# First stage's attention of a two-block model on one core: heads in three steps, and the out projection accumulated per pair of heads

## The chip, the core and the metric

The kernel runs on one core of a Trainium2 chip. The metric is the device time of one execution in microseconds (us), as the median of several runs. TensorE (PE) multiplies matrices into PSUM (eight banks of 128 x 512 fp32 each), ScalarE (ACT) and VectorE (DVE) work on elements, GpSimd (POOL) helps, and SyncE (SP) issues most loads from memory.

## The reference

256 tokens of width 1024 pass a first block of two layers (latent attention "mla", then gated linear attention "gla", each followed by a PEER layer with 16384 experts) and a second block with two kinds of windowed attention and a feed-forward layer. The change is in the first layer's attention:

```
def mla_mixer(x, positions, w_down, g_q_lat, w_uq, g_kv_lat, w_ukv, g_qn, g_kn, w_o):
    down = x @ w_down
    c_q, c_kv = rms_norm(...), rms_norm(...)          # 384 and 256 wide
    q = (c_q @ w_uq).reshape(B, S, 16, 96)
    kv = (c_kv @ w_ukv).reshape(B, S, 16, 64 + 64)
    k = concatenate([kv[..., :64], broadcast(k_rope)], axis=-1)
    v = kv[..., 64:]
    q, k = rms_norm and rope of both
    o = causal_attention(q, k, v)                      # 16 heads, 256 queries, blocks of 128
    return o.reshape(B, S, 16 * 64) @ w_o
h = h + mix;  h = h + peer_ffn(rms_norm(h, ...), ...)
```

## The kernel before

Activations lie transposed, features on partitions and 256 tokens along the free axis; h is 8 rows of 128 features. Most products are made in three passes of fp32r: each operand is split into a high and a low part (`split`: ACT writes hi as a copy, DVE writes lo as the rest), and hi x hi, hi x lo and lo x hi are added in PSUM (`mm3`, lines 109 to 111). A weight block of 512 KB is loaded by SP into a tile raw and split (`wblock`); raw, hi and lo have three buffers each (pool strm, line 32). PSUM is two pools of four banks: tag mm (`c.psum()`) and tag acc (`c.psum_a()`, `c.pa`).

The instructions of an engine don't run in the order of the code: at compile time a planner with a model of the times orders them, earlier code first among those that it holds ready, and hands out free buffers as it goes. `behind` and `c.after` add orders by hand.

`mla` projects down, then K (line 791 makes k_), then Q, whose last products are followed by V's projection (24 passes of 512 columns). k_ is scaled per head by a pass (L880) and a DVE multiplication (L882). Then, per head h: four PE instructions make the scores S (L945 adds the mask in bf16, L947 multiplies in fp32, which the trace shows as two records each), DVE takes two maxima (L953), ACT two exponentials (L959), DVE the reciprocal and the scaling (L961, L964), PE three transposes (L967), ACT copies them to PT (L969), and PE multiplies by V (L971 and L973), with 64 columns of V as weights, into the half of a bank of tag acc that belongs to the head. Per pair of heads m, `split` makes row m of ohi and olo. After all heads, `out_proj` goes over the 8 rows of h: 8 x 3 passes of 256 columns each, then DVE adds to h (L680). Two of the eight blocks of w_o have buffers of their own (woh, wol).

Then the PEER layer begins (`peer_body`): `gain_split` (L136 on ACT, L137 on DVE) makes hi and lo of each row of h, and `proj_first` projects them with the first two blocks of wq at once:

```
    w01 = [c.wblock(wq[h], 1024, 5 + h) for h in range(2)]     # 545; its split stands behind row 5 (6) of gain_split
    c.gain_split(g, ghi, glo)
    p01 = [c.psum_a() for _ in range(2)]
    c.proj_first([p[:, :T] for p in p01], w01, (ghi, glo))
```

The class Accumulate stands in the kernel before too, where the last stage (ffn) alone uses it; its four banks are those of tag acc. `add` makes the 24 passes of one block (lines 234 to 236), but holds the last two blocks (LAST = 2) for `finish`:

```
        c.order = [0, 2, 4, 6, 1, 3, 5, 7]                     # 248
        for i, m in enumerate(c.order):
            for t in self.held:
                self.mm(m, *t)
            a = nc.vector.tensor_tensor(c.h[:, m], c.h[:, m], self.acc[m // 2][:, m % 2], op=OP.add)
            if i >= 2 and out is None:
                c.after[c.order[i - 2]] = [a.ins]
```

Of the kernel before, what the change touches and what calls it, by code (L numbers as in the profile page):

```python
# [5 lines left out]
F32 = mybir.dt.float32  # L6
# [707 lines left out]
def mla(c, v, a):  # L714

    nc, tc = c.nc, c.tc
    with tc.tile_pool(name="mla", bufs=1, reuse_waits="tile") as P:
# [168 lines left out]
        for j, jj in enumerate((4, 0, 1, 5, 2, 3)):  # L886
            w = c.wblock(a["w_uq"][jj], 768)
            for e in range(2):
# [25 lines left out]
                c.tick()  # L914

        V = P.tile([128, 2, 1024], F32, name="V", tag="gsq")
        ws = [c.wblock(a["w_ukv_v"][k], 1024) for k in range(2)]
        for b in range(2):
            for hf in range(2):
                p = c.psum()  # L920
                for k in range(2):
                    t = slice(b * 128, (b + 1) * 128)
                    s = slice(hf * 512, (hf + 1) * 512)
                    c.mm3(p, (lhi[:, 3 + k, t], llo[:, 3 + k, t]), (ws[k][0][:, s], ws[k][1][:, s]), k == 0, k == 1)
                nc.scalar.activation(V[:, b, hf * 512:(hf + 1) * 512], p, AF.Copy, scale=skv[:, b:b + 1])
                c.tick()
        c.tick(9)
        rqh = c.rstd(P, pss[:, :32].rearrange("p (b h) -> p b h", b=2), 96, "rqh", s=sq_, extra=96.0 ** -0.5)

        done = []  # L930
        c.table(AF.Exp, [c.last_sqrt])

        ohi, olo = (P.tile([128, 8, T], F32R, name=n) for n in ("ohi", "olo"))
        for m in range(8):
            po = c.pa.tile([128, 512], F32, name="acc", tag="acc")
            for e in range(2):
                h = 2 * m + e
                r = slice(e * 64, (e + 1) * 64)
                rq = slice(0, 128 if e else 96)
                S = c.psum()  # L940
                for qb in range(2):
                    tq = slice(qb * 128, (qb + 1) * 128)
                    n = 128 * (qb + 1)
                    o = S[:, qb * 128:qb * 128 + n]
                    nc.tensor.matmul(S[:, 256 * qb:256 * qb + 128], identb, cmask, start=True, stop=False,  # L945
                                     skip_group_check=True)
                    nc.tensor.matmul(o, q[rq, h, tq], k_[rq, h, :n], start=False, stop=True, skip_group_check=True)  # L947
                st = P.tile([128, 6], F32, name="st", bufs=6)
                Pm = P.tile([128, 384], F32, name="Pm", bufs=4)
                for qb in range(2):  # L950
                    n = 128 * (qb + 1)
                    sl = slice(qb * 128, qb * 128 + n)
                    nc.vector.tensor_reduce(st[:, qb:qb + 1], S[:, sl], axis=AX.X, op=OP.max)  # L953
                for qb in range(2):
                    n = 128 * (qb + 1)
                    sl = slice(qb * 128, qb * 128 + n)
                    nc.vector.scalar_tensor_tensor(st[:, 2 + qb:3 + qb], st[:, qb:qb + 1], -1.0, rqh[:, qb, h:h + 1],
                                                   op0=OP.mult, op1=OP.mult)
                    nc.scalar.activation(Pm[:, sl], S[:, sl], AF.Exp, bias=st[:, 2 + qb:3 + qb],  # L959
                                         scale=rqh[:, qb, h:h + 1], accum_out=st[:, 4 + qb:5 + qb])  # L960
                nc.vector.reciprocal(st[:, 4:6], st[:, 4:6])  # L961
                for qb in range(2):
                    sl = slice(qb * 128, qb * 256 + 128)
                    nc.vector.tensor_scalar(Pm[:, sl], Pm[:, sl], st[:, 4 + qb:5 + qb], None, op0=OP.mult)  # L964
# [634 lines left out]
```

## Time and profile before

| | |
|---|---|
| time before, median of 3 runs (lowest, highest) | 2219.31 us (2217.12, 2219.76) |
| the profiled execution, whole | 2215.98 us |
| its span, first to last instruction | 2214.2 us |
| instructions in it | 41185 |
| the attention with the out projection, on PE | about 64 to 129 us of the span |

A profile is one execution, recorded by the hardware. Times in rows are counted from the start of its span. PEld is TensorE's loading of weights, which overlaps its multiplications. The end of a matmul in a row is modelled, so that rows of PE overlap; the starts tell how fast it goes.

### The profile page before, as it was taken

The numbers are of one execution on the slowest core, as the hardware profiler recorded it, in microseconds if no ns is written. First come the engines' busy times: TensorE is split into PE (matmuls) and PEld (weight loads), VectorE is DVE, ScalarE is ACT, GpSimd is POOL, SyncE is SP. The second block draws the span as 40 slices with busy tenths as digits, with TensorE's granted clock in tenths as the row PEclk, the third lists the DMA queues.
The fourth block names the chain that finished last, engine by engine and source line by source line (L and its number), as shares of the span: only waits on it lengthen the run. The fifth ranks groups of instructions, "written<-read, shape, count | busy, mean of one in ns | idle before, by whom it ended". The sixth has DMA issues, their size and how long they took to land.

```text
span 2214.2 us, 41185 instructions
## 1 busy us (share of the span) xinstructions
PE 2188.5 (99%) x15545; PEld 2005.4 (91%) x15545; DVE 1654.6 (75%) x4268; ACT 1174.5 (53%) x1984; POOL 173.5 (8%) x243
## 2 busy tenths in 40 slices
PE   8999999999999999999999999999999999999999
PEld 7799999999888888889999999988888888779999
DVE  7779997888555777667999788865577767657665
ACT  7764554555554555566455455555445456445443
POOL 4100000111000111000000011100011132000000
PEclk9999999999999999999999999999999999999999
DMA  4254555555655777445455555565567766305554
GB/s 163 67 191 163 192 190 191 200 196 201 228 193 197 235 242 239 152 142 173 166 188 191 191 196 199 198 232 192 197 226 242 244 181 211 113 33 187 187 185 153
DMA packets 116168, 413.22 MB, mean 187 GB/s; under 512 B 14256, under 2 KB 16120, under 8 KB 115456
## 3 DMA queue, kind: packets, MB, share of 16 engines
q1 hardware_dynamic: 102960, 370.46, 48.9%
q0 software_dynamic: 12176, 39.43, 5.6%
q8 instruction: 122, 2.00, 0.4%
q10 hardware_dynamic: 832, 0.70, 0.1%
q14 instruction: 78, 0.64, 0.1%
HBM read 390.06 MB, written 19.94 MB: 185 GB/s over the span
## 4 chain that ended last, share of the span: by engine, by line
PE 93%; DMA 3%; ACT 2%; DVE 1%; issue 1%; ACTq 0%; SPq 0%; DVEq 0%
PE mm L109 16%; PE mm L111 16%; PE mm L110 16%; PE acc L274 10%; PE acc L272 10%; PE acc L273 10%; PE acc L480 1%; PE acc L481 1%; PE acc L109 1%; PE acc L110 1%; PE acc L111 1%; PE acc L235 1%; PE acc L236 1%; PE acc L234 1%; DMA raw<-in_w_qk 1%; PE mm L1351 1%
## 5 line engine op out<-in xcount | busy, mean ns | idle before, releaser
L94 ACT ACTIVATE hi<-raw 128x1024 fp32r<-128x1024 f32 (+1 forms) x687 | 725.8, 1057 | 850.8 <-PE mm L110 303.2
L95 DVE TENSOR_TENSOR lo<-raw,hi 128x1024 fp32r<-128x1024 f32 (+1 forms) x687 | 839.4, 1222 | 352.3 <-ACT hi L94 349.8
L110 PE MATMUL mm<-x,hi 128*128 128x256 f32 x2856 | 798.8, 280 | 3.1 <-DVE x L137 3.1
L109 PE MATMUL mm<-x,hi 128*128 128x256 f32 x2792 | 790.1, 284 | 7.8 <-ACT x L136 6.5
L111 PE MATMUL mm<-x,lo 128*128 128x256 f32 x2792 | 779.9, 280 | 0.0
L110 PEld LDWEIGHTS mm<-x,hi 128*128 128x128 f32 x2856 | 536.9, 188 | 3.9 <-DVE x L137 3.4
L109 PEld LDWEIGHTS mm<-x,hi 128*128 128x128 f32 x2792 | 524.4, 188 | 11.4 <-ACT x L136 6.5
L111 PEld LDWEIGHTS mm<-x,lo 128*128 128x128 f32 x2792 | 524.8, 188 | 0.0
L274 PE MATMUL acc<-hi,ws 128*128 128x512 f32 x992 | 385.9, 389 | 0.0
L273 PE MATMUL acc<-lo,ws 128*128 128x512 f32 x992 | 385.9, 389 | 0.0
L272 PE MATMUL acc<-hi,ws 128*128 128x512 f32 x992 | 266.1, 389 | 0.0
L274 PEld LDWEIGHTS acc<-hi,ws 128*128 128x128 f32 x992 | 186.2, 188 | 38.7
L272 PEld LDWEIGHTS acc<-hi,ws 128*128 128x128 f32 x992 | 186.2, 188 | 38.5
L273 PEld LDWEIGHTS acc<-lo,ws 128*128 128x128 f32 x992 | 186.2, 188 | 38.6
L441 DVE SCALAR_TENSOR_TENSOR Gs<-iota,Gs 128x17 f32<-128x17 f32 (+1 forms) x480 | 96.4, 255 | 0.9
L484 DVE SCALAR_TENSOR_TENSOR Hs<-acc,Hs 128x256 f32<-128x256 f32 x128 | 53.9, 421 | 54.3 <-PE acc L481 54.3
L519 POOL DMA_DIRECT2D ht<-spill x64 | 46.4, 725 | 600.1 <-DVE wm L521 568.0
L500 POOL DMA_DIRECT2D spill<-ht x64 | 46.6, 728 | 496.4 <-ACT ht L499 496.4
L480 PE MATMUL acc<-oh 128*128 128x128 f16 x512 | 67.7, 220 | 0.0
L485 ACT ACTIVATE Gs<-acc 128x192 f32<-128x192 f32 x128 | 41.9, 327 | 47.3 <-DVE Hs L484 47.3
L481 PE MATMUL acc<-oh 128*128 128x128 f16 x512 | 66.1, 218 | 0.0
L95 DVE TENSOR_TENSOR ws<-Hs,ws 128x256 fp32r<-128x256 f32 x128 | 52.8, 418 | 1.0 <-ACT ws L94 1.0
(450 smaller groups left out, 2867.5 us busy)
## 6 DMA issues: line engine op xcount, KB each, us to landing
raw<-in_u SPq DMA_DIRECT2D x256, 512.0 KB, 3.5
raw<-in_v SPq DMA_DIRECT2D x256, 512.0 KB, 4.3
spill<-ht POOLq DMA_DIRECT2D x64, 256.0 KB, 2.7
ht<-spill POOLq DMA_DIRECT2D x64, 256.0 KB, 3.9
raw<-in_w_gate SPq DMA_DIRECT2D x22, 512.0 KB, 4.2
raw<-in_w_up SPq DMA_DIRECT2D x22, 512.0 KB, 4.0
raw<-in_w_dn SPq DMA_DIRECT2D x22, 512.0 KB, 4.2
raw<-in_wq SPq DMA_DIRECT2D x16, 512.0 KB, 4.5
```

The source lines that it names most:

```text
L94: a = nc.scalar.activation(hi, raw, AF.Copy)
L95: b = nc.vector.tensor_tensor(lo, raw, hi.bitcast(F32), op=OP.subtract)
L109: mm(out, w[0], x[0], start=start, stop=False, skip_group_check=skip)
L110: mm(out, w[0], x[1], start=False, stop=False, skip_group_check=skip)
L111: self.last_mm = mm(out, w[1], x[0], start=False, stop=stop, skip_group_check=skip).ins
L272: mm(o, x[:, 0, t], w[0][:, s], start=(i == 0), stop=False)
L273: mm(o, x[:, 0, t], w[1][:, s], start=False, stop=False)
L274: self.last = [mm(o, x[:, 1, t], w[0][:, s], start=False, stop=(i == self.n - 1)).ins]
L441: nc.vector.scalar_tensor_tensor(scr, iota51[:, :n], bf[:, hk:hk + 1], cidx[:, h, :n], op0=OP.is_equal, op1=OP.mult, accum_out=cx[:, hk:hk ...
L480: nc.tensor.matmul(o, b, a, start=True, stop=False)
L481: nc.tensor.matmul(o, b, l, start=False, stop=True)
L484: nc.vector.scalar_tensor_tensor(hv, pv[:, :zone], 2.0 ** -12, hv, op0=OP.mult, op1=OP.mult)
```

## The change

The projection of V, the heads and the out projection are written as one loop over 16 heads. Step h makes the scores and the softmax of head h (`scores`), the product with V of head h - 2 (`values`) and the transposes of head h - 1 (`turned`). Steps 0 and 1 have a half of V's projection each in the place of `values`. The normalisers of Q (rqh) and the table of the exponential come ahead of it. `values` takes the 128 columns of V that belong to the pair as weights, for each of its heads, into a bank of tag mm; of the 128 rows of the result the 64 that belong to the head are split, so that there are 16 splits of 64 partitions in the place of 8 of 128. The scores, the transposes and the results now share the four banks of tag mm, and the four of tag acc belong to Accumulate: after the second head of a pair, `acc.add` adds that pair's share of the out projection to all 8 rows of h. The first six pairs are added in the loop, the last two in `finish`. The weights w_o are laid out by rows on the host, and each of the 8 blocks goes through `wblock`, one in every second step. The body of `scores` is that of before.

```diff
@@ -912,69 +912,91 @@ def mla
...
+        c.tick(9)
+        rqh = c.rstd(P, pss[:, :32].rearrange("p (b h) -> p b h", b=2), 96, "rqh", s=sq_, extra=96.0 ** -0.5)
+        c.table(AF.Exp, [c.last_sqrt])
         V = P.tile([128, 2, 1024], F32, name="V", tag="gsq")
-        ws = [c.wblock(a["w_ukv_v"][k], 1024) for k in range(2)]
-        for b in range(2):
-            for hf in range(2):
...
+        wv = [c.wblock(a["w_ukv_v"][k], 1024) for k in range(2)]
+        def values_of(hf):
+            for b in range(2):
                 p = c.psum()
...
-        c.tick(9)
-        rqh = c.rstd(P, pss[:, :32].rearrange("p (b h) -> p b h", b=2), 96, "rqh", s=sq_, extra=96.0 ** -0.5)
-        done = []
-        c.table(AF.Exp, [c.last_sqrt])
-        ohi, olo = (P.tile([128, 8, T], F32R, name=n) for n in ("ohi", "olo"))
-        for m in range(8):
-            po = c.pa.tile([128, 512], F32, name="acc", tag="acc")
-            for e in range(2):
...
-                pt = c.pa.tile([128, 512], F32, name="acc", tag="acc")
...
-                nc.tensor.matmul(po[r, 128:256], V[:, 1, hs], PT[:, 256:384], start=True, stop=False,
...
-            c.split(po[:, :T], T, ohi[:, m], olo[:, m])
-            done.append(c.last)
-        out_proj(c, a["mla_w_o"], ohi, olo, P, ("woh", "wol"), {2: done[3], 3: done[5], 4: done[6]})
...
+        Ps, PTs, po = {}, {}, []
+        def scores(h):
+            rq = slice(0, 128 if h % 2 else 96)
+            S = c.psum()
...
+            Pm = Ps[h] = P.tile([128, 384], F32, name="Pm", bufs=4)
...
+        def turned(h):
+            Pm = Ps.pop(h)
+            pt = c.psum()
+            for i in range(3):
+                nc.tensor.transpose(pt[:, i * 128:(i + 1) * 128], Pm[:, i * 128:(i + 1) * 128], c.ident)
+            PT = PTs[h] = c.low.tile([128, 512], F32, name="PT", tag="ow")
+            nc.scalar.activation(PT[:, :384], pt[:, :384], AF.Copy)
...
+        def values(h):
+            m, e = h // 2, h % 2
+            if e == 0:
+                po[:] = [c.psum(), P.tile([128, 2, T], F32R, name="o2", bufs=4)]
+            p, o = po
+            PT, o0, vs = PTs.pop(h), e * T, slice(m * 128, (m + 1) * 128)
+            nc.tensor.matmul(p[:, o0 + 128:o0 + 256], V[:, 1, vs], PT[:, 256:384], start=True, stop=False,
+                             skip_group_check=True)
+            nc.tensor.matmul(p[:, o0:o0 + 256], V[:, 0, vs], PT[:, 0:256], start=False, stop=True,
+                             skip_group_check=True)
+            r = halves[e]
+            c.split(p[r, o0:o0 + T], T, o[r, 0], o[r, 1])
+            if e:
+                acc.add(wo.pop(0), o)
...
+        acc = Accumulate(c, 8)
+        wo = []
+        for h in range(16):
+            scores(h)
+            if h < 2:
+                values_of(h)
+            else:
+                values(h - 2)
+            if h % 2 == 0:
+                wo.append(c.wblock(a["mla_w_o"][h // 2], 1024))
+            if h:
+                turned(h - 1)
+        values(14)
+        turned(15)
+        values(15)
+        acc.finish()
...
@@ -1542,7 +1564,7 @@ def host_arrays
-    a["mla_w_o"] = fm(x["mla_w_o"][0])
+    a["mla_w_o"] = x["mla_w_o"][0].reshape(8, 128, 1024)
```

## Rows read from the trace of the kernel before

**Rows 1.** The page, busy time, share and instructions of each engine.
```profile
PE 2188.5 (99%) x15545; PEld 2005.4 (91%) x15545; DVE 1654.6 (75%) x4268; ACT 1174.5 (53%) x1984; POOL 173.5 (8%) x243
```

**Rows 2.** Busy time in one stretch (columns: engines, PEclk, DMA share, GB/s).
```profile
80.00:100.00 20.00, 20.00 (x126) 13.33 (x124) 16.11 (x85) 15.65 (x53) 0.00 (x0) 1.00 0.01 2
```

**Rows 3.** Timeline of PE, heads in the middle (start, duration, instruction, count).
```profile
73.01 0.23 PE L945 MATMUL mm<-cmask,identb 128*128 128x128 bf16 x1
...
73.71 0.47 PE L880 MATMUL acc<-rkT,sel 128*128 128x256 f32 x1
74.02 0.23 PE L945 MATMUL mm<-cmask,identb 128*128 128x128 bf16 x1
...
79.31 0.49 PE L967 MATMUL acc<-ident,Pm 128*128 128x128 f32 x3
79.63 0.22 PE L945 MATMUL mm<-cmask,identb 128*128 128x128 bf16 x1
...
85.80 0.87 PE L967 MATMUL acc<-ident,Pm 128*128 128x128 f32 x6
86.51 0.22 PE L945 MATMUL mm<-cmask,identb 128*128 128x128 bf16 x1
...
87.48 0.43 PE L971 MATMUL acc<-PT,V 128*64 128x128 f32 x2
...
88.28 0.23 PE L945 MATMUL mm<-cmask,identb 128*128 128x128 bf16 x1
```

**Rows 4.** Timeline of PE, visits to L971: the first, one with two heads, the last.
```profile
80.60 0.43 PE L971 MATMUL acc<-PT,V 128*64 128x128 f32 x2
...
107.19 0.45 PE L971 MATMUL acc<-PT,V 128*64 128x128 f32 x4
...
108.00 0.87 PE L967 MATMUL acc<-ident,Pm 128*128 128x128 f32 x6
...
114.69 0.43 PE L971 MATMUL acc<-PT,V 128*64 128x128 f32 x2
```

**Rows 5.** Timeline of PE, the end of the attention and the out projection.
```profile
115.48 0.38 PE L111 MATMUL mm<-ohi,lo 128*128 128x256 f32 x1
116.03 0.51 PE L109 MATMUL mm<-ohi,woh 128*128 128x256 f32 x2 [0.16 <-ACT ohi L94]
...
120.48 0.28 PE L110 MATMUL mm<-olo,hi 128*128 128x256 f32 x1
121.07 0.38 PE L111 MATMUL mm<-ohi,lo 128*128 128x256 f32 x1 [0.32 <-DVE lo L95]
```

**Rows 6.** Timeline of PE, the first pass of V's projection and the first score.
```profile
64.48 0.40 PE L109 MATMUL mm<-hi,lhi 128*128 128x512 f32 x1
...
71.76 0.23 PE L945 MATMUL mm<-cmask,identb 128*128 128x128 bf16 x1
```

**Rows 7.** Timeline of DVE: scaling of k, two maxima, scaling of Pm, a split.
```profile
65.37 0.74 DVE L882 TENSOR_TENSOR k<-k,acc 96x256 f32<-96x256 f32 x2
...
75.11 0.62 DVE L953 TENSOR_REDUCE st<-mm 128x1 f32<-128x128 f32 x2
...
81.60 0.54 DVE L964 TENSOR_SCALAR Pm<-Pm,st 128x128 f32<-128x128 f32 x2
...
116.01 0.42 DVE L95 TENSOR_TENSOR olo<-acc,ohi 128x256 fp32r<-128x256 f32 x1 [2.39 <-ACT ohi L94]
```

**Rows 8.** Timeline of ACT: a head's first exponential and the copy behind both.
```profile
82.37 0.45 ACT L959 ACTIVATE Pm<-mm,st,rqhy 128x128 f32<-128x128 f32 x1
...
83.34 0.49 ACT L969 ACTIVATE PT<-acc 128x384 f32<-128x384 f32 x1
```

**Rows 9.** Groups by line and form, 64 to 135 us (busy, mean ns, idle before).
```profile
L95 DVE TENSOR_TENSOR lo<-raw,hi 128x1024 fp32r<-128x1024 f32 x10 | 12.2, 1224 | 2.2 <-ACT hi L94 2.1
L94 ACT ACTIVATE hi<-raw 128x1024 fp32r<-128x1024 f32 x9 | 9.5, 1053 | 0.7 <-PE mm L110 0.7
...
L136 ACT ACTIVATE x<-x,vecs 128x256 fp32r<-128x256 f32 x8 | 3.8, 502 | 4.6 <-DVE x L680 4.6
L137 DVE SCALAR_TENSOR_TENSOR x<-x,vecs,x 128x256 fp32r<-128x256 f32 x8 | 3.7, 481 | 0.7 <-ACT x L136 0.6
...
L680 DVE TENSOR_TENSOR x<-x,mm 128x256 f32<-128x256 f32 x8 | 3.1, 416 | 1.3 <-PE mm L111 1.3
```

**Rows 10.** Timeline of DVE, the additions of Accumulate.finish in the last stage.
```profile
2206.04 1.92 DVE L252 TENSOR_TENSOR x<-x,acc 128x256 f32<-128x256 f32 x5 [0.81 <-PE acc L236]
...
2208.98 0.42 DVE L252 TENSOR_TENSOR x<-x,acc 128x256 f32<-128x256 f32 x1 [0.30 <-PE acc L236]
2209.70 0.42 DVE L252 TENSOR_TENSOR x<-x,acc 128x256 f32<-128x256 f32 x1 [0.29 <-PE acc L236]
```

More of the change, by code (lines that the diff above doesn't have):

```diff
@@ L930, in mla @@
-        done = []
-        c.table(AF.Exp, [c.last_sqrt])
-        ohi, olo = (P.tile([128, 8, T], F32R, name=n) for n in ("ohi", "olo"))
-        for m in range(8):
-            po = c.pa.tile([128, 512], F32, name="acc", tag="acc")
-            for e in range(2):
[L937 to L964, printed above, removed]
-                pt = c.pa.tile([128, 512], F32, name="acc", tag="acc")
-                for i in range(3):
-                    nc.tensor.transpose(pt[:, i * 128:(i + 1) * 128], Pm[:, i * 128:(i + 1) * 128], c.ident)
-                PT = c.low.tile([128, 512], F32, name="PT", tag="ow")[:, :384]
-                nc.scalar.activation(PT, pt[:, :384], AF.Copy)
-                hs = slice(h * 64, (h + 1) * 64)
-                nc.tensor.matmul(po[r, 128:256], V[:, 1, hs], PT[:, 256:384], start=True, stop=False,
-                                 skip_group_check=True)
-                nc.tensor.matmul(po[r, 0:256], V[:, 0, hs], PT[:, 0:256], start=False, stop=True,
-                                 skip_group_check=True)
-            c.split(po[:, :T], T, ohi[:, m], olo[:, m])
-            done.append(c.last)
@@ L977, in mla @@
-        out_proj(c, a["mla_w_o"], ohi, olo, P, ("woh", "wol"), {2: done[3], 3: done[5], 4: done[6]})
+        Ps, PTs, po = {}, {}, []
+        def scores(h):
+            rq = slice(0, 128 if h % 2 else 96)
+            S = c.psum()
+            for qb in range(2):
+                tq = slice(qb * 128, (qb + 1) * 128)
+                n = 128 * (qb + 1)
+                o = S[:, qb * 128:qb * 128 + n]
+                nc.tensor.matmul(S[:, 256 * qb:256 * qb + 128], identb, cmask, start=True, stop=False,
+                                 skip_group_check=True)
+                nc.tensor.matmul(o, q[rq, h, tq], k_[rq, h, :n], start=False, stop=True, skip_group_check=True)
+            st = P.tile([128, 6], F32, name="st", bufs=6)
+            Pm = Ps[h] = P.tile([128, 384], F32, name="Pm", bufs=4)
+            for qb in range(2):
+                sl = slice(qb * 128, qb * 256 + 128)
+                nc.vector.tensor_reduce(st[:, qb:qb + 1], S[:, sl], axis=AX.X, op=OP.max)
+            for qb in range(2):
+                sl = slice(qb * 128, qb * 256 + 128)
+                nc.vector.scalar_tensor_tensor(st[:, 2 + qb:3 + qb], st[:, qb:qb + 1], -1.0, rqh[:, qb, h:h + 1],
+                                               op0=OP.mult, op1=OP.mult)
+                nc.scalar.activation(Pm[:, sl], S[:, sl], AF.Exp, bias=st[:, 2 + qb:3 + qb],
+                                     scale=rqh[:, qb, h:h + 1], accum_out=st[:, 4 + qb:5 + qb])
+            nc.vector.reciprocal(st[:, 4:6], st[:, 4:6])
+            for qb in range(2):
+                sl = slice(qb * 128, qb * 256 + 128)
+                nc.vector.tensor_scalar(Pm[:, sl], Pm[:, sl], st[:, 4 + qb:5 + qb], None, op0=OP.mult)
```

3 lines of the change are left out of this document (1 added, 2 removed).

## The prediction, made before the changed kernel ran

> **What bounds the kernel now.** I read the page's busy times first, then the windows of the stage, then PE's timeline through it, start by start, and last what DVE and ACT do there.
>
> PE is busy for 99% of the span [rows 1], and the stretch of the attention is no exception: 20.00 of 20 us, with DVE at 16.11 and ACT at 15.65 [rows 2]. The reader should not stop there, since the end of a matmul is modelled. The starts tell the pace. A score with one scaling pass (L880) behind it takes from 73.01 to 74.02, 1.01 us; a pass of 256 columns in fp32r takes 0.12 (six of them lie between two additions, 2208.98 and 2209.70) [rows 10], so the score alone takes 0.89. Three transposes take 79.31 to 79.63, which is 0.107 for 128 columns [rows 3]. From 85.80 on the same pieces take longer: six transposes 0.71 where 6 x 0.107 is 0.64, a score 0.97 where it was 0.89, and the values of one head 0.80 [rows 3]. Two records of 128 and two of 256 columns would take 2 x 0.107 + 2 x 0.214 = 0.64. So nothing stands still for want of data, but 0.07 + 0.08 + 0.16, about 0.3 us, goes with each visit to the instructions with 64 columns, on the way in, inside, and on the way out. Steady heads cost 0.32 + 0.89 + 0.64 + 0.3 = 2.15 us of PE each, and no engine waits that matters.
>
> Only at the end does PE wait: 0.55 us between 115.48 and 116.03 for the last head's split and 0.59 between 120.48 and 121.07 for a weight block, where 0.12 is the pace; together 0.9 us [rows 5]. The out projection follows the attention on PE with no other gap.
>
> So before any change of order can help, it must take work from PE or fill these 0.9 us. The heads already overlap: the scores at 73.01 to 79.63 run ahead of the first transposes [rows 3].
>
> **The change, part by part.**
>
> *Values with 128 columns.* I count 14 visits of L971 and L973 in PE's timeline, the first at 80.60 and the last at 114.69: twelve with one head and two with two heads at once; in one of these, four records of each start from 107.19 on, and the next transposes at 108.00, 0.81 us for two heads [rows 4]. The change removes 14 x 0.3 = 4.1 us of switching. It loses the two double visits, 2 x 0.64 = 1.3. Saved: 2.8 us. Not shown before is how fp32 weights of 128 columns load in this place. Below, they cost nothing; above, what a score loses against its columns, 0.89 - 6 x 0.107 = 0.25 with two masks in it, some 0.06 for each of four instructions; one such per head gives 16 x 0.06 = 0.9. I take +0.4.
> The row shows two heads sharing the array in the time of one. The Trainium skill (TensorEngine Tiling (Array Packing), section Overview) states the same as a rule: a dimension of 64 or less allows up to twice the speed by tiling. By that rule the step goes the wrong way, 16 x 0.64 = 10.2 us against 8 x 0.8 = 6.4; by the rows, two pairs of eight had it.
>
> *Out projection by pairs.* 192 passes before and after, each 0.12: nothing on PE. In the loop each `acc.add` needs the split of its pair's second head: 0.43 us above the pace for hi [rows 5], lo 0.42 later [rows 7]. Cover: the transposes of the next head (0.32) and the scores of the one after (0.89), if a bank is free. With it, nothing; without the scores, 0.43 - 0.32 for hi plus what lo adds, up to 0.5, for six pairs: 3 us. I take +0.9, nearer to nothing, because scores did run ahead of transposes [rows 3].
>
> *Other engines.* ACT per pair: exponentials 2 x 0.97 (82.37 to 83.34), copies 2 x 0.49, splits 2 x 0.4, one weight block 1.05: 4.8 us [rows 8, 9]. DVE: maxima 2 x 0.62, scaling 2 x 0.54, splits 2 x 0.42, a weight block 1.22 [rows 7, 9], and some 0.8 of short operations: 5.2. PE per pair: 2 x (0.89 + 0.32 + 0.64) + 24 x 0.12 = 6.6. The eight additional splits (0.4 on each engine) hide under PE; without that cover they would cost 3.3 us.
>
> *V's projection and rqh.* The 24 passes are the same and run where PE has little else: before, they begin at 64.48, and the first score comes at 71.76 [rows 6]. The first two heads' k is scaled by 66.1 [rows 7]. If the planner keeps to the written order, PE waits up to 66.1 - 64.5 = 1.6 us for score 0; it has V's first half as filler, so I take nothing. The exponentials may start some 2 us earlier, as the two splits into woh and wol leave the queues ahead of them; PE does not wait for that.
>
> *Loads.* SP issues the same eight blocks of 512 KB, in the same place of its queue (behind V's two, ahead of PEER's first). Each needs a raw buffer, which the split of the third block before it frees, a pair of heads or 6.6 us apart; DMA is nearly idle there (share 0.01) [rows 2]. Cost: nothing.
>
> *The drain.* Behind the last score: maxima 0.62, exponentials 0.97, scaling 0.54, transposes 0.32, copy 0.49, values 0.64, split 0.55 [rows 5, 7, 8], 4.1 us, and about 0.5 of short steps by estimate: 4.6. PE's work in it: values 13 and 14 and transposes 14 (1.6), its own 0.96, and pair 6 in `finish`. Of that pair only rows 0, 2, 4 and 6 can go ahead (12 x 0.12 = 1.4); rows 1, 3, 5 and 7 lie in banks that DVE reads next. Idle: 4.6 - 4.0 = 0.6, and up to 1.9 if pair 6 itself comes late. I take 1.2.
>
> *The handover to PEER.* `finish` gives h back within 3.7 us (first addition 2206.04, last 2209.70 in the last stage) [rows 10], where `out_proj` took some 2.9 us per row. Per row DVE has an addition (0.42) and L137 (0.48) to do, ACT L136 (0.50) [rows 9]: 8 x 0.9 = 7.2 us of DVE in 3.7. And of the three buffers of hi and lo two hold blocks 6 and 7 until the end of `finish`; wq's first two blocks must be split behind rows 5 and 6 of h, and row 5 is now seventh in the order. So a block of wq is ready at the earliest 1.05 + 1.22 us [rows 9] after a buffer falls free 0.3 us ahead of the end: PE, which has nothing else, waits 2.0. Bounds: 0.5 if the third buffer goes to wq early, 3.9 if DVE does all rows of h first. Then the 48 passes of two blocks (5.8 us) cover the rest.
>
> **Sum.** -2.8 + 0.4 - 0.9 (both waits of rows 5 are gone) + 0.9 + 1.2 + 2.0 = +0.8 us. The profiled execution took 2215.98 us (span 2214.2 and 1.8 around it), so 2216.8; the median is 3.3 above the profiled one, so about 2220 us beside 2219.31. Less than 0.2% (4.4 us) is about what cannot be told from no change here.
>
> **Rivals.**
>
> 1. *The planner fills the end* with rows of h and an early block of wq, so that drain and handover cost next to nothing: -2.8 + 0.4 - 0.9 = -3.3, 2216.0 in the median. For it: it interleaves finely. Against it: all three buffers are taken.
>
> 2. *PE has more room than its starts show*, and a loop written for it finds it. Loads of weights (PEld) fill only 13.33 of the 20 us of steady heads [rows 2]; the other 6.7 us recovered would make 2212.6. For it: that gap. Against it: a record of 256 columns streams for 0.214 us and its load is shorter, so the gap is no wait. The Trainium skill (Perfetto Trace Analysis, section Identifying the Most-Contended Engine) reads TensorE's headroom from the busy share of its weight loads, which would make this rival the forecast.
>
> 3. *Slower: PSUM.* Scores, transposes and results shared eight banks with the out projection idle; now they have four, a result holding one for two steps. If no bank is free for the next scores, each pair's addition waits for its split, 0.43 + 0.42, with a late copy or split 1.1 us: 8 x 1.1 = 8.8 in the place of the 0.9 taken. Net +8.7, 2228. It decides from about four pairs on (0.8 - 0.9 + 4 x 1.1 = 4.3).
>
> 4. *The order does nothing.* The planner's order was already a pipeline, and only the switches and the handover count: -2.8 + 0.4 - 0.9 + 2.0 = -1.3, 2218.
>
> **How the numbers follow.** Forecast 0.45 (2217.5 to 2223), rival 1 0.15, rival 2 0.12, rival 3 0.18, rival 4 0.10. Where rival 1 holds and the exponentials' earlier start gives another 2 us, the time is also below 2214.9: 0.02 of its 0.15. Faster by over 0.2%: 0.12 + 0.02 = 0.14; slower: 0.18 and 0.01 from the forecast's top, 0.19; within: 0.67. The range leaves out rival 2 and the worse half of rival 3: 2214 to 2226.
>
> **What would show it.** L971 and L973 as 128*128, a head's values in 0.64 to 0.7 us, scores at 0.89 throughout. No gap over 0.3 us ahead of L234 between heads (rival 3: a gap at each pair, ended by ACT or DVE `o2`). One gap of about a microsecond before the last pair, one of about two between the last L236 and the first pass with wq, ended by DVE lo. If PE stands still before the first transposes, the start was misjudged; if the switches stay, the first term is wrong.

## The result, and the profile after

The changed kernel took 2232.24 us (median of 4 runs, 2230.59 to 2236.42), the kernel before, run beside it, 2219.53 (2217.12 to 2220.02): 1.0056 times as long, 95% interval 1.0041 to 1.0071. It is slower, 12 us above the forecast of 2220 and 6 above its range. The profiled execution took 2230.59 us (span 2228.9).

Most of the loss lies in one stage; the two spans differ by 14.7 us (2214.2 and 2228.9). ACT's copy into rkT, the last row ahead of it that all kernels share, starts at 57.66 before and 57.92 after; the next stage's first copy into ht at 347.80 and 360.92. The way between them went from 290.14 to 303.00, 12.86 us more. I call this difference *the stage's loss* below. It is taken from one execution of each kernel, and that of the kernel before (2215.98 us, mean granted clock 1.000) was faster than each of its four timed ones.

The page's busy times answer to [rows 1]: PE works longer for the same 15545 instructions.

```profile
PE 2194.3 (98%) x15545; PEld 2014.8 (90%) x15545; DVE 1660.8 (75%) x4276; ACT 1179.8 (53%) x1992; POOL 172.4 (8%) x243
```

The windows through the stage (columns as in [rows 2]) say where. PEclk is 1.00 before; here it is 0.93, 0.81 and 0.91 in three windows. A window's share at half clock is twice what is missing: 2.8 + 7.6 us from 60 to 100, and 3.6 from 140 on. Elsewhere PE is idle at full clock (16.34 from 120 to 140).

```profile
60.00:80.00 20.00, 17.36 (x107) 15.10 (x107) 16.87 (x45) 16.55 (x34) 7.77 (x8) 0.93 0.41 130
80.00:100.00 20.00, 19.42 (x120) 17.05 (x119) 11.36 (x44) 11.53 (x33) 0.00 (x0) 0.81 0.18 55
...
120.00:140.00 20.00, 16.34 (x118) 14.33 (x117) 13.28 (x42) 12.49 (x32) 0.00 (x0) 1.00 0.08 26
140.00:160.00 20.00, 19.30 (x148) 19.09 (x149) 12.91 (x16) 11.86 (x18) 0.59 (x1) 0.91 0.69 237
```

**The start.** PE's timeline, from the last scaling of k to the first heads' values (to [rows 3, 6, 7]):

```profile
75.08 1.04 PE L880 MATMUL acc<-rkT,sel 128*128 128x256 f32 x3 [0.15 <-DVE k L882]
78.61 0.45 PE L963 MATMUL mm<-ident,Pm 128*128 128x128 f32 x1 [2.49 <-DVE Pm L957]
...
81.77 0.79 PE L974 MATMUL mm<-PT,V 128*128 128x128 f32 x2 [0.58 <-ACT PT L965]
...
85.56 0.85 PE L963 MATMUL mm<-ident,Pm 128*128 128x128 f32 x3
86.20 0.63 PE L974 MATMUL mm<-PT,V 128*128 128x128 f32 x2
```

PE stands for 2.49 us, then 0.58, and three transposes take 0.64 (85.56 to 86.20) where they took 0.32 [rows 3]: half pace. What it waits for is the first scaling on DVE, and that is not later than before (79.31 was the first transpose there [rows 3]). By these rows the difference is what PE had to do until then: I count 14 records of the mask's pass, seven heads' scores, ahead of the first transposes before, and 4, two heads, after. DVE ahead of the scaling, then ACT ahead of the first exponential:

```profile
74.60 1.41 DVE L882 TENSOR_TENSOR k<-k,acc 128x256 f32<-128x256 f32 x4 [0.36 <-PE acc L880]
75.94 1.22 DVE L95 TENSOR_TENSOR lo<-raw,hi 128x1024 fp32r<-128x1024 f32 x1
77.07 0.74 DVE L882 TENSOR_TENSOR k<-k,acc 128x256 f32<-128x256 f32 x2
...
78.20 0.98 DVE L957 TENSOR_SCALAR Pm<-Pm,st 128x128 f32<-128x128 f32 x4
```

```profile
73.78 1.06 ACT L94 ACTIVATE hi<-raw 128x1024 fp32r<-128x1024 f32 x1 [0.20 <-PE mm L111]
74.75 0.44 ACT L952 ACTIVATE Pm<-mm,st,rqhy 128x128 f32<-128x128 f32 x1
```

Both carry a split of a w_o block (1.22 and 1.06) in the middle of the first softmax.

**The pairs in the middle** go as forecast: from the out projection of one pair to that of the next 6.70 us (forecast 6.6), no wait ahead of L234, visits to the values without a switch.

```profile
102.62 0.82 PE L234 MATMUL acc<-o,hi 128*128 128x256 f32 x4
...
107.22 0.49 PE L974 MATMUL mm<-PT,V 128*128 128x128 f32 x2
107.54 0.60 PE L976 MATMUL mm<-PT,V 128*128 128x256 f32 x2
...
109.32 0.70 PE L234 MATMUL acc<-o,hi 128*128 128x256 f32 x3
```

**The drain and the handover** (to [rows 5]):

```profile
129.50 0.75 PE L234 MATMUL acc<-o,hi 128*128 128x256 f32 x4 [0.47 <-ACT o L94]
...
132.68 0.74 PE L234 MATMUL acc<-o,hi 128*128 128x256 f32 x4 [0.47 <-ACT o L94]
...
137.00 0.28 PE L236 MATMUL acc<-o,lo 128*128 128x256 f32 x1
140.25 0.39 PE L109 MATMUL acc<-x,hi 128*128 128x256 f32 x1 [2.97 <-ACT hi L94]
...
141.20 0.39 PE L109 MATMUL acc<-x,hi 128*128 128x256 f32 x1 [0.45 <-ACT hi L94]
```

ACT splits three blocks of wq in a row, 1.9 us behind the end of w_o's last pass (137.28):

```profile
137.00 0.51 ACT L136 ACTIVATE x<-x,vecs 128x256 fp32r<-128x256 f32 x1 [0.22 <-DVE x L252]
137.41 1.04 ACT L158 ACTIVATE Hs<-x 128x1024 f32<-128x1024 f32 x1
138.36 0.89 ACT L136 ACTIVATE x<-x,vecs 128x256 fp32r<-128x256 f32 x2
139.16 2.94 ACT L94 ACTIVATE hi<-raw 128x1024 fp32r<-128x1024 f32 x3
```

By these rows it is not the buffers that come last. Block 5 left its buffer when pair 5 had been added (its last pass starts at 125.71), the other two are free from 137.28 on, and no load is under way from 125 to 140 (DMA share 0.00). What stands ahead of the first split is ACT's work on seven of the eight rows of h (L136) and a copy into Hs: the code puts that split behind row 5, the seventh in the order.

In sum: idle 2.49 + 0.58 + 0.47 + 0.47 + 2.97 + 0.45 = 7.4 us, some 0.2 more for each of the six, since a pass is shown that much longer than its pace, 8.6; rows at half pace from 78.61 to 87.5, 8.9 us with 0.6 of idle in them, so up to 4.1; behind the handover 3.6 us at half clock, so up to 1.8. That is 14.5 at most; less the 2.8 and 0.9 saved it is 10.8, of 12.86 found.

### The profile page after: what moved, and what is told of

Same layout as the page of the kernel before. It is cut to its first block, busy times and chain, and to the rows that moved or that the text cites. A ratio compares the mean times of both kernels' runs of the same rounds, so it can differ in the third digit from the quotient of the medians.

```text
span 2228.9 us, 41207 instructions
## 1 busy us (share of the span) xinstructions
PE 2194.3 (98%) x15545; PEld 2014.8 (90%) x15545; DVE 1660.8 (75%) x4276; ACT 1179.8 (53%) x1992; POOL 172.4 (8%) x243
## 4 chain that ended last, share of the span: by engine, by line
PE 93%; ACT 2%; DMA 2%; DVE 2%; issue 1%; ACTq 0%; DVEq 0%
PE mm L109 16%; PE mm L111 16%; PE mm L110 16%; PE acc L272 10%; PE acc L273 10%; PE acc L274 10%; PE acc L480 1%; PE acc L481 1%; PE acc L234 1%; PE acc L235 1%; PE acc L236 1%; PE acc L109 1%; PE acc L111 1%; PE acc L110 1%; PE mm L1373 1%; ACT hi L94 1%
```

## The experiments

Each ratio is to the kernel before, run on the same chip beside it. The medians quoted below come from several chips, so that kernels are best compared by their ratios. The stage's loss comes from the profiled execution alone, as above. In the twelve kernels marked * V's first pass stands 1.2 to 1.6 us further behind ACT's copy into rkT than in the others with the same place of V (own buffers 8.85 us, changed 7.30), so that this much of their column is no work of the edits. In these twelve, and in no other, the granted clock is at its lower level for some stretch between 48 and 64 us.

| kernel | ratio, 95% interval | stage's loss, us |
|---|---|---|
| changed | 1.0056, 1.0041 to 1.0071 | 12.86 |
| V first * | 1.0072, 1.0059 to 1.0086 | 18.10 |
| own buffers * | 1.0029, 1.0020 to 1.0039 | 10.55 |
| both of these | 1.0070, 1.0054 to 1.0087 | 16.22 |
| late splits * | 1.0058, 1.0042 to 1.0074 | 9.53 |
| late splits, own buffers * | 1.0043, 1.0029 to 1.0057 | 10.89 |
| all three | 1.0044, 1.0030 to 1.0057 | 9.16 |
| narrow values * | 1.0082, 1.0069 to 1.0096 | 16.91 |
| pipeline only * | 1.0005, 0.9993 to 1.0018 | 1.99 |
| accumulation only * | 1.0324, 1.0299 to 1.0348 | 72.64 |
| accumulator later | 1.0043, 1.0030 to 1.0056 | 12.88 |
| accumulator later, own buffers * | 1.0039, 1.0026 to 1.0051 | 9.06 |
| filler | 1.0044, 1.0030 to 1.0059 | 10.92 |
| filler, own buffers | 1.0033, 1.0020 to 1.0046 | 8.82 |
| start as before, V first * | 1.0046, 1.0032 to 1.0059 | 11.14 |
| start as before, V between * | 1.0031, 1.0017 to 1.0044 | 7.95 |
| before, wide values * | 0.9996, 0.9986 to 1.0007 | 1.67 |
| before, wide, last pair narrow * | 0.9994, 0.9985 to 1.0003 | 1.77 |
| the same without scalings | 0.9985, 0.9974 to 0.9996 | -1.01 |

My theory after the trace was A: the loss sits at the two ends, because V's projection stands between the heads and wq's buffers are taken. Rivals were a shortage in every pair (B) and the pipeline's own order (C); after the first results A2 took A's place at the start (splits of w_o in the first softmax), and D joined, the accumulation.

**V first.** V's products, each with its tick, and rqh go ahead of the heads:

```
+        for hf in range(2):
+            values_of(hf)
         c.tick(9)
...
-            if h < 2:
-                values_of(h)
-            else:
+            if h > 1:
                 values(h - 2)
```

> The changed kernel, but with both halves of V's projection ahead of the heads again, as before the change; pipeline, 128-column values and accumulated out projection stay. Theory A (the loss sits at the two ends of the stage): the hole of 2.9 us ahead of the first transposes and the 10.24 us at half clock behind it (some 4 us) go, so 7 us less than the changed kernel: 2224 to 2226 us, and the granted clock is full from 60 to 130 us. Theory B (the pairs run short of PSUM buffers, or the accumulation costs in each pair): the hole goes but what it cost comes back in the pairs, at most 2 us less: 2230 to 2232 us. Theory C (the pipeline's order itself starves TensorE at its start, whatever V does): the stall stays between the first scores and the first transposes, with the half clock, and the time is that of the changed kernel or worse.

2236.46 us, more than the changed kernel (the ratios' intervals overlap): A and B missed, and C had this side. PE's rows at the start:

```profile
81.47 0.38 PE L880 MATMUL acc<-rkT,sel 128*128 128x256 f32 x1 [0.92 <-DVE k L882]
82.33 0.38 PE L880 MATMUL acc<-rkT,sel 128*128 128x256 f32 x1 [0.48 <-DVE k L882]
84.32 1.31 PE L880 MATMUL acc<-rkT,sel 128*128 128x256 f32 x3 [1.61 <-DVE k L882]
87.07 0.45 PE L967 MATMUL mm<-ident,Pm 128*128 128x128 f32 x1 [1.44 <-DVE Pm L961]
```

The wait is split into four, and longer: 4.45 us idle. Two splits of w_o now fall between DVE's multiplications of k. So V between the heads was not the fault, and A fell at the start.

**Own buffers.**

```
-    w01 = [c.wblock(wq[h], 1024, 5 + h) for h in range(2)]
+    w01 = [c.wblock(wq[h], 1024, 5 + h if c.order[1] == 1 else None) for h in range(2)]
...
+        hl = [P.tile([128, 2, 1024], F32R, name=n, tag=n) for n in ("woh", "wol")]
...
-                wo.append(c.wblock(a["mla_w_o"][h // 2], 1024))
+                raw = c.load_block(a["mla_w_o"][h // 2], 1024)
+                wo.append(c.split(raw, 1024, *([t[:, h // 2 - 6] for t in hl] if h >= 12 else [])))
```

> The changed kernel, but the last two blocks of w_o are split into buffers of their own and the first two blocks of wq wait for no buffer row, so that the shared weight buffers are free for wq before the out projection has ended. Theory A: 3.7 us lost between the last out projection pass and the first dense passes with wq fall to 1 us or less, and the 3.4 us at half clock (1.6 us) go with them: 4 us less than the changed kernel, 2227 to 2228.5 us. Rival: wq's splits wait for their load, or ScalarE and VectorE are the ones that are late, and the gap stays above 3 us: 2231 to 2233 us.

2226.73 us, as A had it. The edit lifts two limits at once, the buffers and the place behind rows 5 and 6, so that it doesn't tell them apart; ACT's rows above speak for the second. The wait is gone from PE's timeline:

```profile
142.14 0.28 PE L236 MATMUL acc<-o,wol 128*128 128x256 f32 x1
142.27 0.36 PE L109 MATMUL acc<-x,hi 128*128 128x256 f32 x1
```

The stage's loss fell by 2.3 only, by 3.9 without the 1.55 that came ahead of V's first pass. And this execution has two new waits among the pairs (1.13 and 1.64 us from start to start). Just ahead of each ACT splits a block into the new buffers, many pairs before it is used:

```profile
100.67 1.06 ACT L94 ACTIVATE woh<-raw 128x1024 fp32r<-128x1024 f32 x1 [0.60 <-DMA raw<-in_mla_w_o]
...
108.12 1.06 ACT L94 ACTIVATE woh<-raw 128x1024 fp32r<-128x1024 f32 x1 [2.01 <-DMA raw<-in_mla_w_o]
```

**Both edits.**

> Both of the edits above in one: V's projection ahead of the heads, and own buffers for the last two blocks of w_o. Theory A: the two gains add up, 11 to 12 us less than the changed kernel, 2219 to 2221 us, level with the kernel before. If the two ends are not independent (a later start only shifts what the second end waits for), the sum of the two single gains is missed by 2 us or more. Theory B: 2229 us or more.

2234.09: the gains don't add up (A: 2219 to 2221), and V first costs here no less than alone (7.4 us beside 4.2).

**Late splits of w_o** (mark[h]: the last exp and scaling of head h):

```
-                wo.append(c.wblock(a["mla_w_o"][h // 2], 1024))
+                with c.behind(mark[h] if h else []):
+                    wo.append(c.wblock(a["mla_w_o"][h // 2], 1024))
```

> The changed kernel, with one edit: from the second block of w_o on, a block's two splits are issued behind the last exp and the last scaling of the head at whose step the block is loaded, so that none of them can stand ahead of the first head's softmax except block 0's. Theory A2 (the first transposes are late because VectorE and ScalarE take splits of w_o, 1.2 and 1.06 us each, ahead of the first heads' softmax): the hole of 2.9 us ahead of the first transposes shrinks by 1.2 to 2.3 us, and if TensorE's clock then stays up, 4 us more go: 2225 to 2231 us. Theory C (the order of the steps starves TensorE there, because the second score tile's successor has no PSUM buffer until V's last half is copied out): the hole stays over 2.5 us and the time is that of the changed kernel, 2231 to 2233 us.

2229.92, in A2's range. In the rows A2 was right too: PE's wait fell from 2.49 to 0.96, and no half clock followed (window 80 to 100: 1.00). The time hardly shows it; in this execution the fall behind the handover was longer (window 130 to 150).

```profile
79.16 0.30 PE L964 MATMUL mm<-ident,Pm 128*128 128x128 f32 x1 [0.96 <-DVE Pm L957]
...
81.14 0.49 PE L975 MATMUL mm<-PT,V 128*128 128x128 f32 x2 [0.58 <-ACT PT L966]
```

```profile
80.00:100.00 20.00, 18.03 (x130) 16.05 (x129) 14.29 (x50) 13.71 (x38) 0.00 (x0) 1.00 0.22 69
130.00:150.00 20.00, 16.41 (x113) 15.55 (x111) 14.07 (x25) 11.50 (x19) 0.58 (x1) 0.83 0.38 132
```

**With own buffers, and all three:**

> The late splits of w_o and the own buffers for its last two blocks together. Own buffers alone gave 5.5 us. Theory A2: both gains add, 2219 to 2225 us. Theory C: as with own buffers alone, 2226 to 2228 us.

> V's projection ahead of the heads, own buffers for the last two blocks of w_o, and its other splits late. Without the late splits this kernel took 2234 us, with four holes of 0.9 to 2.0 us on TensorE between the first scores and the first transposes, in which VectorE ran two splits of 1.2 us and the 16 additions that complete the keys. Theory A2: the two splits gone from there take 2 to 3 us of holes and some of the half clock with them: 2226 to 2231 us. If the additions to the keys alone are what holds the first softmax up: 2232 to 2235 us, and V's projection belongs between the heads, where the change put it.

2228.47 and 2228.51: no sum of gains in the first, against A2 (own buffers alone had 2226.73), and the late splits take 5.6 us from the kernel with the other two edits (2234.09). Between 2226 and 2229 these runs rank nothing.

**Narrow values** (the change without its wide weights):

```
-            PT, o0, vs = PTs.pop(h), e * T, slice(m * 128, (m + 1) * 128)
-            nc.tensor.matmul(p[:, o0 + 128:o0 + 256], V[:, 1, vs], PT[:, 256:384], start=True, stop=False,
+            PT, o0, vs, r = PTs.pop(h), e * T, slice(h * 64, (h + 1) * 64), halves[e]
+            nc.tensor.matmul(p[r, o0 + 128:o0 + 256], V[:, 1, vs], PT[:, 256:384], start=True, stop=False,
```

> The changed kernel with the values taken at 64 columns of V, each head into its half of the partitions, as before the change. Prediction's sum for this part: 14 to 16 visits with a switch of the weights' width come back at some 0.3 us each, less 0.4 us: 2.5 to 4 us above the changed kernel, 2234.5 to 2236.5 us, with the values of a head at 0.9 us or more where the changed kernel has 0.65. Rival: the narrow weights cost nothing between dense work, and the time is within 1 us of the changed kernel.

2237.97, above the forecast. From the first transposes to the first pass with wq PE takes 65.86 us (84.45 to 150.31) where the changed kernel takes 61.64, 4.2 us more, and from one pair's out projection to the next 7.53 (110.10 to 117.63) where it takes 6.70. In the changed kernel the wide values are worth what the prediction said, or more.

**The two halves apart.** The pipeline without the accumulation (transposes and values in tag acc, `out_proj` behind the heads):

```
-            pt = c.psum()
+            pt = c.pa.tile([128, 512], F32, name="acc", tag="acc")
...
-            c.split(p[r, o0:o0 + T], T, o[r, 0], o[r, 1])
-            if e:
-                acc.add(wo.pop(0), o)
+            c.split(p[r, o0:o0 + T], T, ohi[r, m], olo[r, m])
```

> The change without the accumulated out projection: the three-step pipeline over heads, V's projection between the heads and the 128-column values stay, and the out projection is again the separate one behind the heads, with transposes and values in the PSUM tag acc as before the change. Theory D (the loss comes from the accumulation: it holds all four acc banks from the first head on, so that scores, transposes, values and V share the four mm banks, and it brings w_o's splits to the start and to the end): the holes at the start, in the drain and at the handover are gone, the clock stays up, and what is left is the gain of the wide values, 1.5 to 3 us: 2216 to 2219 us. Theory C (the order of the steps is what starves TensorE at the start): the hole of 2 to 3 us ahead of the first transposes and the half clock behind it stay: 2224 to 2228 us.

And the accumulation in the kernel before, without the pipeline:

```
+        acc = Accumulate(c, 8)
         for m in range(8):
+            wo = c.wblock(a["mla_w_o"][m], 1024)
-            po = c.pa.tile([128, 512], F32, name="acc", tag="acc")
+            po = c.psum()
...
+            c.split(po[:, :T], T, o[:, 0], o[:, 1])
+            acc.add(wo, o)
+        acc.finish()
```

> The kernel before, with the out projection accumulated per pair of heads alone: V's projection ahead of the heads, no pipeline, 64-column values; transposes and values in tag mm, since the accumulation holds acc. Theory D: most of the loss is here, 2230 us or more: as with V first in the changed kernel, but with no steps in between two heads' waits. Theory C: without the pipeline the accumulation fills the gaps between heads and the time is at most that of the kernel before plus the 3.7 us of the handover, 2219 to 2224 us.

2223.55 beside 2221.81, ratio 1.0005: the pipeline costs nothing. It does not bring the gain that D promised either (2216 to 2219). The accumulation alone: 2294.4, 72 us more. PE's timeline for one pair of it:

```profile
119.38 0.30 PE L967 MATMUL mm<-ident,Pm 128*128 128x128 f32 x1 [2.96 <-DVE Pm L964]
...
121.79 0.69 PE L971 MATMUL mm<-PT,V 128*64 128x128 f32 x2 [0.64 <-ACT PT L969]
...
123.80 1.22 PE L234 MATMUL acc<-o,hi 128*128 128x256 f32 x4 [0.47 <-ACT o L94]
```

PE stands through one softmax per pair (2.9 to 3.0 us each time), which fits a full PSUM, and the clock falls again and again (0.71 in this window):

```profile
80.00:160.00 80.00, 56.41 (x264) 42.17 (x264) 26.55 (x95) 24.38 (x66) 0.00 (x0) 0.71 0.10 34
```

So the accumulation is a loss of some 72 us that the rest of the change wins back but for 12. D holds here, C falls.

**The accumulator later** (taken at the first addition; two heads' transposes in acc), alone and with own buffers:

```
-            pt = c.psum()
+            pt = c.psum() if h > 1 else c.pa.tile([128, 512], F32, name="acc", tag="acc")
...
+                if m == 0:
+                    acc.append(Accumulate(c, 8))
```

> The changed kernel with one edit: the accumulator's four acc banks are taken at the first pair's addition instead of ahead of the heads, and the first two heads' transposes go into the acc tag, so that mm has a bank for the next scores while TensorE waits for the first softmax. If it is PSUM that leaves TensorE without work there (theory D), the hole of 2.9 us ahead of the first transposes falls to under 1.5 us and the clock's fall behind it goes: 4 to 6 us less than the changed kernel, 2225 to 2228 us. If VectorE's and ScalarE's splits of w_o hold the first softmax up whatever TensorE has (A2), more scores go first and the first transposes are as late as they were: 1 to 2 us less at most, 2229 to 2232 us.

> The later accumulator and own buffers for the last two blocks of w_o together. Own buffers alone gave 5.5 us less than the changed kernel (2226.7). If the two ends are independent and D holds at the start: 2220 to 2223 us. If the start's loss stays: 2225 to 2227 us.

2232.22 and 2230.98, the second above both its forecasts: one more head's score went ahead, and the first transposes were as late (two waits, 1.35 and 1.49 us). Two banks do not do it.

**Filler.** Passes that nothing uses keep PE busy while it would wait:

```
+        def fill(n, ins):
+            with c.behind([ins]):
+                for _ in range(n):
+                    nc.tensor.matmul(acc.acc[0][:, 0], lhi[:, 0, :128], lhi[:, 0], start=True, stop=True,
+                                     skip_group_check=True)
...
+            if h == 1:
+                fill(21, c.last_mm)
```

> The changed kernel with work added that nothing uses: 21 passes of 256 columns (0.118 us each, 2.5 us) between the last addition to the keys and the first transposes, and 6 more ahead of the first head's values, into an acc bank that the first out projection pass clears. The attention waits as long as it did, but TensorE is not idle. If the half clock of 10.24 us behind the hole is a price of its own, it goes: the granted clock is full from 70 to 130 us and the time is 3 to 5 us less than the changed kernel's, 2226 to 2229 us. If it was not the idle TensorE that lowered the clock, or if the half clock is hidden behind waits for the softmax anyway, the time is the changed kernel's or up to 1 us more: 2230 to 2233 us.

> The same added work, with own buffers for the last two blocks of w_o. With own buffers alone: 2226.7 us, at full clock from the pairs on. If the half clock at the start has a price of its own: 2222 to 2224 us, with the hole of 2.9 us, that of 1 us, and the drain still in it. If not: 2226 to 2228 us.

2230.05 and 2228.13, on the side of a half clock that hides behind other waits. But the windows of the first show full clock where the changed kernel had 0.93 and 0.81, with the transposes at the same 78.6:

```profile
60.00:80.00 20.00, 19.84 (x133) 17.61 (x132) 16.85 (x45) 16.48 (x35) 7.75 (x8) 1.00 0.38 131
80.00:100.00 20.00, 19.29 (x142) 17.22 (x141) 13.84 (x51) 13.31 (x38) 0.00 (x0) 1.00 0.18 59
```

```profile
75.98 2.77 PE L962 MATMUL acc<-lhi 128*128 128x256 f32 x21
78.59 0.27 PE L969 MATMUL mm<-ident,Pm 128*128 128x128 f32 x1
```

The idle PE did lower the clock, and the price was 1.9 us of the stage (12.86 to 10.92), not 4: at full clock PE came to the next wait sooner (0.98 us from start to start at 84.3). The Trainium skill (Perfetto Trace Analysis, section Matmul Optimizations) says that TensorE's power follows its use, so that matmuls should run back to back; these two windows agree.

**The start as before.** The first two pairs' transposes and values in acc, the accumulator at the third pair, w_o one pair later, own buffers:

```
-            pt = c.psum()
+            pt = c.psum_a() if h < 4 else c.psum()
...
+                if m == 2:
+                    acc.append(Accumulate(c, 8))
+                while acc and ready:
+                    acc[0].add(wo.pop(0), ready.pop(0))
```

> Own buffers for the last two blocks of w_o, V's projection ahead of the heads, and the first two pairs kept out of the accumulation: their transposes and values go into the acc tag, their splits are held, each block of w_o comes one pair later, and the accumulator is taken at the third pair, which adds all three. So mm holds scores alone while the first softmax runs. If the start's loss is that TensorE has only two or three heads' scores to do there (theory D), the holes ahead of the first transposes fall under 0.5 us in sum, no half clock follows, and what stays is the drain (1.3 us) and a microsecond of the handover: 2219 to 2222 us. If the loss is moved to the third pair, where three additions wait for the accumulator's banks and for three splits of w_o: 2225 us or more.

> The same with V's projection between the first two heads, as the change has it. By theory D V's position is then of no weight: within 1.5 us of the kernel with V first, 2219 to 2223 us. If V between the heads is a loss of its own (its four results pass through the mm banks that the scores need), 2 us or more above it.

2231.12 with V first, as the second theory had it, and 2227.53 with V between, which neither forecast had. Six heads' scores do run ahead now, and in the second kernel full clock follows. Yet the waits come back one by one behind them, for DVE and ACT:

```profile
81.75 0.30 PE L963 MATMUL acc<-ident,Pm 128*128 128x128 f32 x1 [0.77 <-DVE Pm L957]
...
83.27 0.49 PE L974 MATMUL acc<-PT,V 128*128 128x128 f32 x2 [0.58 <-ACT PT L965]
...
85.53 0.46 PE L974 MATMUL acc<-PT,V 128*128 128x128 f32 x2 [0.92 <-DVE st L950]
...
87.52 0.33 PE L963 MATMUL mm<-ident,Pm 128*128 128x128 f32 x1 [0.77 <-DVE Pm L957]
```

With one of 0.20 that is not shown they make 3.2 us; the two waits of the changed kernel made 3.1. So PSUM decides where PE waits at the start, but not how long in sum; that the sum is the softmax's own time is the likely reading, not a shown one. By the stage's loss V between the heads is the better place here too (7.95 beside 11.14; the ratios' intervals overlap).

**Wide values in the kernel before.** First all pairs, then the last one narrow, last without the softmax's reciprocal and scalings:

```
-                nc.tensor.matmul(po[r, 128:256], V[:, 1, hs], PT[:, 256:384], start=True, stop=False,
+                nc.tensor.matmul(po[:, o0 + 128:o0 + 256], V[:, 1, vs], PT[:, 256:384], start=True, stop=False,
...
-            c.split(po[:, :T], T, ohi[:, m], olo[:, m])
+                c.split(po[r, o0:o0 + T], T, ohi[r, m], olo[r, m])
```

> The kernel before with one part of the change alone: each head's values take the 128 columns of V that its pair owns, and each head's half is split by itself; V first, the order of the heads and the separate out projection stay. Prediction's sum for this part: 4.1 us of switches between 128- and 64-column weights less, 0.4 us of wider weights and up to 1.3 us back from visits that were only one switch: 2.5 to 3 us below the kernel before, 2216.5 to 2217.5 us. Rival: the waits of the values' rows were waits for PT, not switches of the weights' shape; then the rows with 128 columns last as long as they did and the time is within 1 us of the kernel before.

> The kernel before with 128-column values for the first seven pairs, and for the last pair 64 columns and one split of both heads as before. With all pairs wide a wait of 0.86 us stood behind the last pair's second split, where the kernel before waits 0.54 us; in rows the wide values took 1.7 us less. If the two are independent: 1.3 to 2 us below the kernel before, ratio 0.9991 to 0.9994. If the saving is taken up elsewhere (by the splits of half a pair on ScalarE and VectorE, twice as many): ratio 0.9997 to 1.0005.

> The kernel before with wide values for seven pairs and the last narrow, and with the division by the row sums left out (the reciprocal and the two scalings of each head, 0.54 us of VectorE and some short steps per head), so the attention's weights are not normalized. With wide values the switches of 0.31 us were gone from TensorE's rows, but waits of 0.4 to 0.65 us for an exponential (ScalarE behind VectorE's maxima) stood in their place. If the softmax on VectorE and ScalarE paces the heads as much as TensorE does, the waits shrink to under 0.3 us and the saving of the wide values comes out at last: 2 to 4 us below the kernel before, ratio 0.9982 to 0.9991. If the waits come from the order of the instructions or from PSUM, they stay, and the time is that of the same kernel with the scalings: ratio 0.9992 to 1.0003.

0.9996, 0.9994 and 0.9985. The second lies in the range of the first forecast, but its interval takes in the second forecast and 1.0 as well: a gain of 1 us is neither shown nor excluded. In the second kernel (timeline and window) the switches are gone from the seven wide pairs, and scores wait for an exponential instead; DVE is at 18.36 of 20:

```profile
84.36 0.22 PE L945 MATMUL mm<-cmask,identb 128*128 128x128 bf16 x1 [0.27 <-ACT Pm L959]
```

```profile
80.00:100.00 20.00, 18.84 (x129) 16.20 (x129) 18.36 (x94) 16.81 (x58) 0.00 (x0) 1.00 0.01 2
```

Half of DVE's additional 2.25 us is the change's own doing, since a split comes with each head now and not with each pair (DVE's groups from 80 to 100 us, before and here):

```profile
L95 DVE TENSOR_TENSOR olo<-acc,ohi 128x256 fp32r<-128x256 f32 x4 | 1.7, 417 | 0.0
```

```profile
L95 DVE TENSOR_TENSOR olo<-acc,ohi 64x256 fp32r<-64x256 f32 x7 | 2.9, 417 | 0.2
```

Without the scalings DVE falls to 13.53 in that window, those waits are gone, and the stage is 1.0 us shorter than before: the first kernel here that is faster, by leaving work out.

```profile
80.00:100.00 20.00, 19.31 (x139) 17.05 (x138) 13.53 (x53) 19.22 (x64) 0.00 (x0) 1.00 0.02 5
```

No version with all the work beat the kernel before.

## Why the prediction was wrong

- *The step that failed: "V's projection and rqh", "so I take nothing".* It asked whether PE waits for the first score, not what PE has to do while the first softmax runs. Before, seven heads' scores; after, two. The reason is PSUM, which Accumulate holds half of from the first head on. It cost 3.1 us idle and up to 4.1 of half clock, of which 1.9 are shown (filler). V's place isn't it (V first is no better). With six heads' scores ahead again (start as before, V between) the one long wait and the half clock are gone, but waits of 3.2 us stay. The prediction itself named the sign: "If PE stands still before the first transposes, the start was misjudged".
- *The handover, 2.0 taken, 0.5 to 3.9 as bounds:* the wait came and within its bounds, but it was mis-sized, 3.4 idle. The 2.0 counted from the moment when a buffer falls free; in the rows the first split stands behind row 5 of h, nearly the upper bound's case (DVE does all rows first), and one buffer had long been free. A fall of the clock behind it was in no bound. The edit that gave own buffers and lifted that order removed both.
- *The drain, 1.2:* two waits of 0.47, some 1.3 with their pace. Right.
- *Pair additions, +0.9:* near zero; the pairs run at 6.70 us.
- *Switches, -2.8:* gone as said, and their undoing costs 4.2 up to the handover. But the sentence ahead of it, "no engine waits that matters", was wrong for the kernel before: there DVE and ACT, with the softmax and the splits, are about as slow as the heads on PE, so that the wide values alone gain nothing measurable.
- *Rival 3* had the side, the cause and nearly the time (2228), but in the wrong place: no pair in the middle waits for its split; PSUM is short at the start. Its 8.8 us were eight waits that did not come, so that its nearness is luck. *Rival 2* fell: the pairs run at the pace of the starts (6.70 beside 6.6), and PEld's gap was no room. *Rival 4*'s ground, that the order does nothing, is what the pipeline without the accumulation shows (1.0005). *Rival 1* fell: nothing filled the end.
- *Open:* of the 12.86 us some 2.1 have no row of their own, and 4.3 if the half clock at the start is put at its net 1.9. Why late splits and own buffers together do no better than own buffers alone isn't settled either; that the early splits into the new buffers hold up the softmax there is argued from their place alone.

## What to carry to other kernels

When an accumulator takes banks for a whole loop, list what used them to run ahead, and ask what TensorE does during the first softmax, not only in the steady pairs. A gap on TensorE at the start or the end of a stage can cost more than its length, since the clock may fall behind it. Before work is taken off an engine that looks 100% busy, add up the next one's share of the same stage: at 16 of 20 us, and with one more split per pair, DVE was at 18.36 as soon as the switches were gone. Before a wait is put down to a buffer, look at what the waiting engine does when the buffer falls free.

## What the runs showed of the hardware

The granted clock fell to its lower level (1.2 of 2.4 GHz; transposes 0.213 us apart where they were 0.107) behind TensorE's wait of 2.49 us and behind that of 2.97 us; the windows show 10.4 and 3.6 us of it. A wait alone does not settle it: with late splits the first wait was 0.96 us and the window from 80 to 100 us was at full clock; with own buffers added it was the same 0.96 us, and that window had 0.83. Ahead of V's projection a stretch at the lower level cost 1.5 us: in own buffers the granted clock is 0.66 from 58 to 63 us (1.00 in the changed kernel), which is 3.4 us at the lower level with PE busy for 4.63 of the 5, and V's first pass comes 1.55 us later behind the copy into rkT. The kernel before has falls too: over the 97 runs of it that stood beside the experiments the mean granted clock and the time go together, 2218.9 us (median) in the 24 at 0.999 or more, 2226.0 in the 15 at 0.994 or less. That spread, and not the edits, is likely what makes the intervals above as wide as they are.
